# One decoder step on one core: the order of loads and combinations in the output projection, the order of the memory attention's matmuls, two splits through PSUM, and POOL's sums in halves

## The chip, the core and the metric

The kernel runs on one core of a Trainium2 chip. A core has a matmul engine (TensorE, here PE, whose weight loads are listed as PEld), a vector engine (VectorE, DVE), an activation engine (ScalarE, ACT), a general engine (GpSimd, POOL) and a queue engine that mostly issues transfers (SyncE, SP). Each works through its own list of instructions in order, and waits on semaphores for the others. SBUF is the on-chip memory, PSUM the smaller one into which PE accumulates. The metric is the device time of one execution in microseconds (us), lower is better.

## What is computed

One inference step of a decoder layer, for a prompt of 512 tokens and 8 sample sequences of 4 tokens (544 columns in all, handled as two halves of 272):

```python
def decoder_layer(x, s0, k_buf, v_buf, mem_k, mem_v, lb, ...):
    y, s_new, k_new, v_new = token_mixer(rmsnorm(x, norm_mix_w), s0, k_buf, v_buf, ...)
    x = x + y                                   # ends with concat([a_out, b_out]) @ w_out
    x = x + memory_attend(rmsnorm(x, norm_xattn_w), mem_k, mem_v, w_mq, w_mo)
    x = x + swiglu(rmsnorm(x, norm_ffn_w), w_gate, w_up, w_down)
```

The token mixer projects x, runs a gated recurrence with 8 heads (HGRN) and sliding-window attention side by side, and projects both together with w_out (2048 x 2048). The memory attention has 4 heads of 128 over 256 memory rows for the prompt and over caches for the samples, and a projection w_mo from 512 to 2048. The feed-forward part has 5632 hidden units. All is in float32.

## The kernel before

**Products.** A float32 product is made as three products of rounded operands: each operand is split into a high part (a cast on ScalarE) and a low part (the rest, a subtraction on VectorE), and PE does high x high, high x low and low x high. The large projections are in addition done with seven block products in place of eight: `B11, B21, T2, T1, T3, B22, T4` of `QO`, whose weight operands are blocks A11, A21, A12, A22 of the weight matrix and their combinations S1, S2, S3 and A12 less S2, and whose data operands are blocks of the columns and combinations of them.

**Stages.** Input projection with the HGRN heads in between (`hgrn_head`, which puts other work between its own steps with `draw(n)`: n matmuls of whatever stands in the list `line`), then the output projection, the memory attention, its projection w_mo (called mo), gate and up, down, final norm. Each of these lays its operands down while the stage before still runs.

**Output projection** (`out_unit`). A unit is one quarter of the output columns (o4) of one half of the inner dimension: rows1 with o4 = 0, 2, 3, 1, then rows2 with 2, 3, 0, 1. It loads its four blocks through `load` (512 KB each, SP's queue, tiles `oraw`), makes S1, S2, S3 on POOL with `comb` (tiles `ocomb`), and then, product by product, splits the weights (`ohi` and `oh2` on ScalarE, `olo` on VectorE), lets PE do 24 matmuls, and adds the result into x. Blocks come from pool `wr` with 4 buffers, but A22, once the second half is under way, from pool `wx` with 2. While the unit o4 = 1 of rows1 runs, its hook `rows2_parts` builds the data operands of rows2: `Rows` makes a combination into `ot1` and one into `mix0` on POOL (L634, L635), `part` splits each operand (`split`, L606 on ScalarE and L607 on VectorE) and makes two more combinations (L645, L647). In the units of rows2 the hook `beside` prepares operands of the memory attention. The order of each engine's list comes from a scheduler, out of the program's order and the waits that it expects, not from the order of the code alone.

**Memory attention.** Query projections `mq` for four heads and two halves stand in `line`; the scores of each follow after `draw` calls. The first units of mo stand in `line` too, so that they can run between the last heads. `add_mo(i, half)` is one unit of mo: 24 matmuls over three part products (`at`) and four heads (k), then the addition into x (DVE, L1556), the square (`sqt`) and its sum, on POOL for the first half (`SS`, L1562) and on VectorE for the second (`SW`).

**Operands of gate and up** (`ffn_parts`). After the units of mo that finish two rows of x, the data operands are made: `B11` and `B21` with their high part on ScalarE (`ffn_w`) and their low part on VectorE (L1583), further ones f and t (L1535, L1589) on VectorE and POOL. `norm_rows` makes the norms' factors in two halves, each with `rsqrt`, which loads ScalarE's table set first.

Of the kernel before, what the change touches and what calls it, by code (L numbers as in the profile page):

```python
# [10 lines left out]
F32 = mybir.dt.float32  # L11
# [8 lines left out]
P = 128  # L20
# [24 lines left out]
def hybrid_step(ctx: ExitStack, tc: tile.TileContext, a):  # L45
# [863 lines left out]
    def hgrn_head(h):  # L909
# [7 lines left out]
        qp = hg.tile([P, TT], F32, tag="qp", name="qp")  # L917
        nc.gpsimd.tensor_tensor(qp, q, f, ALU.mult)
        step()
        draw(8)  # L920


        A = hg.tile([P, NB, P], F32, tag="A", name="A")
# [160 lines left out]
    def out_unit(rows, o4, old, hook=None):  # L1084

        n0 = o4 * 4 * P

        def load(f, c, last=False):
            p, n = (wx[0], 2) if rows2_on and last else (wr, 4)
            t = p.tile([P, WCH * P], F32, tag="raw", name="oraw", bufs=n)  # L1090
            t = t.rearrange("p (k c) -> p k c", k=DN)
            c0 = n0 + c * 2 * P
            dma(t, w_out[f * P : (f + DN) * P, c0 : c0 + 2 * P].rearrange("(k p) c -> p k c", p=P))
            return t

        def comb(x, y, op):
            t = wst.tile([P, WCH * P], F32, tag="raw", name="ocomb", bufs=3)
            t = t.rearrange("p (k c) -> p k c", k=DN)
            nc.gpsimd.tensor_tensor(t, x, y, op)
            return t  # L1100

        f0 = rows.g * 4
        A11, A21, A12, A22 = load(f0, 0), load(f0, 1), load(f0 + DN, 0), load(f0 + DN, 1, True)

        def run():
            S1 = comb(A21, A22, ALU.add)
            S2 = comb(S1, A11, SPLIT)
            S3 = comb(A21, A11, SPLIT)
            accs = [acc_tile("o_ps") for _ in range(2)]
            if next(units_made) % 2:  # L1110
                accs.reverse()
            o, x = (
                {
                    q: y[:, 2 * i : 2 * i + 2, t]
                    for q, (i, t) in dict(c11=(0, T0), c12=(0, T1), c21=(1, T0), c22=(1, T1)).items()
                }
                for y in (old, X[o4])
            )
            for i, (q, src, bank, first, dst, fresh) in enumerate((
                ("B11", A11, 0, True, "c11", True), ("B21", A12, 1, True, "c11", False),  # L1120
                ("T2", S2, 0, False, "c12", True), ("T1", S1, 1, True, "c22", True),
                ("T3", S3, 0, False, "c22", False), ("B22", None, 1, False, "c12", False),
                ("T4", A22, 0, False, "c21", True),
            )):
                rows.part(i)
                if src is None:
                    src = comb(A12, S2, SPLIT)
                hi = wst.tile([P, WCH * P], F32R, tag="hi", name="ohi")
                lo = wst.tile([P, WCH * P], F32R, tag="lo", name="olo")
                hi, lo = (t.rearrange("p (k c) -> p k c", k=DN) for t in (hi, lo))  # L1130
                if heads_done:
                    for j in range(2):
                        js = slice(2 * j, 2 * j + 2)
                        h2 = ps_to[0].tile([P, 2, 2 * P], F32R, tag="to"[j], name="oh2")
                        if j == 0:
                            nc.scalar.copy(hi, src)
                        nc.scalar.copy(h2, src[:, js])
                        nc.vector.tensor_tensor(lo[:, js], src[:, js], h2.bitcast(F32), SPLIT)  # L1138
                else:
                    split(hi, lo, src)  # L1140
                rows.part(i + 1)
                if hook:
                    hook(i)
                xh, xl = rows.ops[q]
                acc = accs[bank]
                for wt, xt_, at in ((hi, xh, 0), (hi, xl, 1), (lo, xh, 2)):
                    for p in range(2):
                        s = slice(p * P, (p + 1) * P)
                        for k in range(DN):
                            nc.tensor.matmul(  # L1150
                                acc[:, p, :HT], wt[:, k, s], xt_[:, k],
                                start=first and k + at == 0, stop=k == DN - 1 and at == 2,
                                skip_group_check=True,
                            )
                            if at != 1 or k % 2:
                                yield
                add(x[dst], (o if fresh else x)[dst], acc[:, :, :HT])

        return run()
# [67 lines left out]
    def norm_rows(out, sums, tag="t"):  # L1227

        for (b, e), s in zip(HALF, sums):
            pt = ps("nr_ps", tag)[:, : TT // 2]  # L1230
            n = s.shape[1]
            for u in range(n):
                nc.tensor.matmul(pt, ones, s[:, u], start=u == 0, stop=u == n - 1)
            v = small.tile([P, TT], F32, tag="nv", name="nv", bufs=1)[:, : TT // 2]
            nc.vector.tensor_scalar(v, pt, 1.0 / D, EPS, ALU.mult, ALU.add)
            t = small.tile([P, TT], F32, tag="sqt", name="nt", bufs=2)[:, : TT // 2]
            rsqrt(out[:, b:e], v, t)

    rows2 = []

# [263 lines left out]
    for n, u in enumerate(units):  # L1504
        need(("mq", *u))
        if n:
            x_turn(*units[n - 1])
            draw(4)
        else:
            draw(36)  # L1510
        x_scores(*u)
        draw(14)
        if n:
            x_values(*units[n - 1])
        for _ in range(6 if n >= MH - 1 else 0):
            x_more(1)
            draw(5)
# [21 lines left out]
    def add_mo(i, half, done=None):  # L1539


        def run():
            if i not in mo_w:
                mo_w[i] = [next(wparts) for _ in range(MH)]
            acc = acc_tile("mo_ps")
            for at in range(3):
                for k, hi, lo in mo_w[i]:
                    wt, xt_ = (hi, hi, lo)[at], ox[half][k][at % 2]
                    for u in range(2):
                        nc.tensor.matmul(  # L1550
                            acc[:, u, :HT], wt[:, u * P : (u + 1) * P], xt_,
                            start=k + at == 0, stop=k == MH - 1 and at == 2,
                        )
                        yield
            x = X[i // 2][:, 2 * i % 4 : 2 * i % 4 + 2, (T0, T1)[half]]
            nc.vector.tensor_tensor(x, x, acc[:, :, :HT], ALU.add)  # L1556
            if i == 0:
                nc.scalar.activation(S3[half], x, AF.Square)
            else:
                t = post.tile([P, 2, HT], F32, tag="sqt", name="sqt", bufs=2)  # L1560
                nc.scalar.activation(t, x, AF.Square)
                (nc.vector if half else nc.gpsimd).tensor_add(S3[half], S3[half], t)  # L1562
            if done:
                done(i)

# [9 lines left out]
    def ffn_parts(i):  # L1575
# [3 lines left out]
        for u, q in enumerate(("B11", "B21")):  # L1579
            o = 2 * i + u  # L1580
            hi, lo = (t[:, i] for t in fops[q])
            ffn_w(hi, o, T0)
            nc.vector.scalar_tensor_tensor(  # L1583
                lo, xt(o)[:, T0], vcol("ffn", o), hi.bitcast(F32), ALU.mult, SPLIT
            )
        t1 = ap.tile([P, HT], F32, tag="t1", name="t1", bufs=2)
        t2 = ap.tile([P, HT], F32, tag="t2", name="t2")
# [545 lines left out]
```

## Time and profile before

| | |
|---|---|
| median of 3 runs | 2591.98 us (2590.53 to 2594.45) |
| the profiled execution | 2587.27 us, span 2585.5 us, mean granted clock 0.993 |
| PE busy | 2511.4 us, 97 % of the span |
| VectorE, ScalarE, POOL busy | 66 %, 60 %, 43 % |
| output projection | about 780 to 974 us of the span |
| memory attention and mo | about 974 to 1136 us |

The span runs from the first to the last instruction. All times of rows below are in us from its start, within this one execution. A number in square brackets at the end of a row is the time for which the engine had been idle, with what ended the wait.

### The profile page before, as it was taken

What the parts mean: (1) busy time and instruction counts of PE and PEld (TensorE: products, weight loads), DVE (VectorE), ACT (ScalarE), POOL (GpSimd) and SP (SyncE); (2) the same over time, 40 slices, a digit from 0 to 9 for tenths busy, and PEclk for the clock granted to TensorE, in tenths of its full rate; (3) what the DMA queues carried; (4) which work ended last, traced back from release to release, by engine and by line L of the source; (5) the groups of instructions that cost most, each with busy time, mean ns of one, the idle gap of its engine ahead of it and who ended that gap; (6) DMA issues with size and microseconds to landing.
All of it is one profiled execution on the core that took longest, in us unless ns stands there. A gap on an engine that the chain in (4) does not pass through costs nothing.

```text
span 2585.5 us, 48037 instructions
## 1 busy us (share of the span) xinstructions
PE 2511.4 (97%) x19679; PEld 2443.3 (95%) x19679; DVE 1708.9 (66%) x2560; ACT 1557.7 (60%) x2181; POOL 1104.3 (43%) x643
## 2 busy tenths in 40 slices
PE   8999999999999999989999999999999999999997
PEld 7999999998998998779999999999999999999987
DVE  5555655565559796497666666666666676777887
ACT  5343223333327685467677777777776778767767
POOL 4101122122125631165555555555555566665752
PEclk9999999999999999999999999999999999999999
DMA  7222323554524226523333333333333453333325
GB/s 240 83 68 82 91 83 92 152 149 143 182 66 135 91 73 186 187 93 107 116 107 117 114 123 113 122 115 113 116 107 116 142 211 133 101 131 133 116 70 164
DMA packets 287164, 315.44 MB, mean 122 GB/s; under 512 B 9508, under 2 KB 239220, under 8 KB 284097
## 3 DMA queue, kind: packets, MB, share of 16 engines
q1 hardware_dynamic: 273024, 264.80, 32.2%
q0 software_dynamic: 13920, 47.58, 5.6%
q8 instruction: 155, 2.54, 0.4%
q14 instruction: 65, 0.52, 0.1%
HBM read 278.28 MB, written 33.64 MB: 121 GB/s over the span
## 4 chain that ended last, share of the span: by engine, by line
PE 54%; DVE 6%; ACT 3%; issue 2%; DMA 2%; POOL 1%; ACTq 0%; DVEq 0%; POOLq 0%; SPq 0%
PE s_ps L1703 48%; PE o_ps L1150 3%; PE d_ps L1987 1%; PE mq_ps L1445 1%; DVE slo L1647 1%; DMA wraw<-in_w_down_dram 1%; DVE wlo L132 1%; ACT shi L1645 0%; ACT h L1646 0%; DVE x L1887 0%; DMA xkv<-in_cache_mem_v_dram 0%; POOL scomb L1665 0%; DVE olo L1138 0%; DMA wraw<-in_w_mq_dram 0%; PE xk_ps L1363 0%
## 5 line engine op out<-in xcount | busy, mean ns | idle before, releaser
L1647 DVE TENSOR_TENSOR slo<-scomb,h 128x1024 fp32r<-128x1024 f32 x256 | 312.5, 1221 | 243.2 <-ACT h L1646 232.8
L1645 ACT CAST shi<-scomb 128x1024 fp32r<-128x1024 f32 x256 | 269.2, 1052 | 190.8 <-PE s_ps L1703 168.9
L131 ACT CAST whi<-wraw 128x1024 fp32r<-128x1024 f32 (+1 forms) x204 | 169.4, 845 | 342.0 <-PE in_ps L345 278.4
L1665 POOL TENSOR_TENSOR scomb<-sraw 128x1024 f32<-128x1024 f32 (+1 forms) x134 | 319.4, 2386 | 7.5 <-DVE slo L1647 2.5
L1665 POOL TENSOR_TENSOR scomb<-sraw,scomb 128x1024 f32<-128x1024 f32 (+1 forms) x67 | 166.5, 2486 | 327.9 <-DVE slo L1647 319.3
L1645 ACT CAST shi<-sraw 128x1024 fp32r<-128x1024 f32 x192 | 201.6, 1050 | 160.9 <-issue 99.5
L345 PE MATMUL in_ps<-xh,whi 128*128 128x272 f32 x1280 | 276.6, 297 | 0.8 <-ACT whi L131 0.8
L345 PE MATMUL in_ps<-xl,whi 128*128 128x272 f32 x1280 | 274.2, 295 | 0.0
L345 PE MATMUL in_ps<-xh,wlo 128*128 128x272 f32 x1280 | 272.1, 294 | 0.9 <-DVE wlo L132 0.8
L132 DVE TENSOR_TENSOR wlo<-wraw,whi 128x1024 fp32r<-128x1024 f32 (+1 forms) x204 | 208.0, 1033 | 96.6 <-ACT whi L131 92.1
L1646 ACT CAST h<-scomb 128x1024 fp32r<-128x1024 f32 x256 | 258.6, 1010 | 3.1 <-DVE slo L1647 3.0
L1647 DVE TENSOR_TENSOR slo<-sraw,h 128x1024 fp32r<-128x1024 f32 x192 | 233.8, 1218 | 28.0 <-ACT h L1646 23.2
L345 PEld LDWEIGHTS in_ps<-xh,whi 128*128 128x128 f32 x1280 | 201.8, 189 | 6.6 <-issue 4.3
L345 PEld LDWEIGHTS in_ps<-xh,wlo 128*128 128x128 f32 x1280 | 201.9, 189 | 6.4 <-issue 4.4
L345 PEld LDWEIGHTS in_ps<-xl,whi 128*128 128x128 f32 x1280 | 202.0, 189 | 5.1 <-issue 4.4
L1646 ACT CAST h<-sraw 128x1024 fp32r<-128x1024 f32 x192 | 194.1, 1011 | 17.8 <-DVE slo L1647 17.6
L1703 PE MATMUL s_ps<-T,shi 128*128 128x272 f32 x1408 | 191.9, 288 | 0.9 <-DVE T L607 0.5
L1703 PEld LDWEIGHTS s_ps<-T,shi 128*128 128x128 f32 x1408 | 182.8, 188 | 1.5 <-ACT T L606 0.8
L611 DVE TENSOR_TENSOR gu<-gu,s_ps 128x272 f32<-128x272 f32 x264 | 111.3, 435 | 109.4 <-PE s_ps L1703 106.8
L1703 PE MATMUL s_ps<-dT,shi 128*128 128x272 f32 x1280 | 173.8, 288 | 2.7 <-ACT h L1646 1.4
L1703 PEld LDWEIGHTS s_ps<-dT,shi 128*128 128x128 f32 x1280 | 165.1, 188 | 3.6 <-ACT h L1646 1.6
L1665 POOL TENSOR_TENSOR scomb<-scomb,sraw 128x1024 f32<-128x1024 f32 (+1 forms) x67 | 160.4, 2395 | 4.2
(523 smaller groups left out, 5723.6 us busy)
## 6 DMA issues: line engine op xcount, KB each, us to landing
sraw<-in_w_gate_dram SPq DMA_DIRECT2D x44, 1024.0 KB, 5.1
sraw<-in_w_up_dram SPq DMA_DIRECT2D x44, 1024.0 KB, 5.1
wraw<-in_w_in_dram SPq DMA_DIRECT2D x84, 512.0 KB, 4.0
sraw<-in_w_down_dram SPq DMA_DIRECT2D x40, 1024.0 KB, 5.2
oraw<-in_w_out_dram SPq DMA_DIRECT2D x32, 512.0 KB, 3.9
h_d<-gu POOLq DMA_DIRECT2D x22, 544.0 KB, 4.6
wraw<-in_w_mk_dram SPq DMA_DIRECT2D x16, 512.0 KB, 3.7
wraw<-in_w_mv_dram SPq DMA_DIRECT2D x16, 512.0 KB, 3.9
```

Source lines behind the costliest of these rows:

```text
L131: nc.scalar.copy(hi[:, s], raw[:, s])
L132: nc.vector.tensor_tensor(lo[:, s], raw[:, s], hi[:, s].bitcast(F32), SPLIT)
L345: nc.tensor.matmul(acc[:, i, : e - b], wt, xt[:, b:e], start=j + at == 0, stop=j == KD - 1 and at == 2,)
L611: nc.vector.tensor_tensor(out, x, y, ALU.add)
L1150: nc.tensor.matmul(acc[:, p, :HT], wt[:, k, s], xt_[:, k], start=first and k + at == 0, stop=k == DN - 1 and at == 2, skip_group_check=True,)
L1445: nc.tensor.matmul(acc, wt, xt_, start=j + at == 0, stop=j == KD - 1 and at == 2)
L1645: first = nc.scalar.copy(hi, src)
L1646: nc.scalar.copy(h2, src)
L1647: return first, nc.vector.tensor_tensor(lo, src, h2.bitcast(F32), SPLIT)
L1665: ins = nc.gpsimd.tensor_tensor(t[:, p], x[:, p], y[:, p], op)
L1703: nc.tensor.matmul(accs[p], wt[:, k, s], xt_[:, k], start=k + at == 0, stop=k == n - 1 and at == 2,)
L1987: nc.tensor.matmul(acc[:, 0, : e0 - b0], (hi, hi, lo)[at], hp[k][at % 2][:, b0:e0], start=k + at == 0, stop=k == nf - 1 and at == 2,)
```

## The change

Seven places are changed.

- HGRN heads 0 and 7 draw 16 matmuls in place of 8 at one of their steps.
- In units of the output projection with a hook, A22 is loaded third and from pool `wr`, A12 fourth. Units without one keep their order.
- The instructions that a hook makes on POOL are put behind the instruction that makes S3 (`tc.issue_after(summed.ins)` ties those of the same engine alone).
- The second half of each norm in `norm_rows` no longer loads the table set.
- The memory attention draws 47 matmuls in place of 36 ahead of the first scores.
- The first two units of mo order their 24 matmuls by head, and by part product within a head.
- `ffn_parts` writes the high parts of B11 and B21 a second time, into PSUM, and the splits on VectorE read them there; POOL's sums of squares are made in two halves of 272 columns.

```diff
-        draw(8)
+        draw(8 if 0 < h < H - 1 else 16)
...
-            nc.gpsimd.tensor_tensor(t, x, y, op)
-            return t
+            return t, nc.gpsimd.tensor_tensor(t, x, y, op)
...
-        A11, A21, A12, A22 = load(f0, 0), load(f0, 1), load(f0 + DN, 0), load(f0 + DN, 1, True)
+        A11, A21 = load(f0, 0), load(f0, 1)
+        if hook:
+            A22 = load(f0 + DN, 1)
+            A12 = load(f0 + DN, 0)
+        else:
+            A12, A22 = load(f0 + DN, 0), load(f0 + DN, 1, True)
...
-            S1 = comb(A21, A22, ALU.add)
-            S2 = comb(S1, A11, SPLIT)
-            S3 = comb(A21, A11, SPLIT)
+            S1, _ = comb(A21, A22, ALU.add)
+            S2, _ = comb(S1, A11, SPLIT)
+            S3, summed = comb(A21, A11, SPLIT)
...
-                    hook(i)
+                    with tc.issue_after(summed.ins):
+                        hook(i)
...
-            rsqrt(out[:, b:e], v, t)
+            rsqrt(out[:, b:e], v, t, preload=b == 0)
...
-            draw(36)
+            draw(47)
...
-            for at in range(3):
-                for k, hi, lo in mo_w[i]:
-                    wt, xt_ = (hi, hi, lo)[at], ox[half][k][at % 2]
-                    for u in range(2):
...
+            order = [(at, part) for at in range(3) for part in mo_w[i]]
+            if done is None and i < 2:
+                order.sort(key=lambda o: o[1][0])
+            for n, (at, (k, hi, lo)) in enumerate(order):
...
-                (nc.vector if half else nc.gpsimd).tensor_add(S3[half], S3[half], t)
+                if half:
+                    nc.vector.tensor_add(S3[half], S3[half], t)
+                else:
+                    for u in range(2):
+                        nc.gpsimd.tensor_add(S3[half][:, u], S3[half][:, u], t[:, u])
...
+            h2 = ps_to[0].tile([P, 512], F32R, tag="to"[u], name="b2")[:, :HT]
+            ffn_w(h2, o, T0)
             ffn_w(hi, o, T0)
             nc.vector.scalar_tensor_tensor(
-                lo, xt(o)[:, T0], vcol("ffn", o), hi.bitcast(F32), ALU.mult, SPLIT
+                lo, xt(o)[:, T0], vcol("ffn", o), h2.bitcast(F32), ALU.mult, SPLIT
             )
```

**Where instructions stand.** POOL in the output projection, before the change: 8850 to 8856 are the blocks of the unit o4 = 3 of rows1, 9108 to 9114 those of o4 = 1, and A22 of the latter is 9114.

```order
L634 TENSOR_TENSOR ot1_9167<-mix0_406 128x1088
L635 TENSOR_TENSOR mix0_406<-mix0_406,mix1_407 128x4x272
L645 TENSOR_TENSOR mix0_406<-mix0_406 128x4x272
L1099 TENSOR_TENSOR ocomb_8858<-oraw_8852,oraw_8856 128x1024
L1099 TENSOR_TENSOR ocomb_8860<-ocomb_8858,oraw_8850 128x1024
L1099 TENSOR_TENSOR ocomb_8862<-oraw_8852,oraw_8850 128x1024
L1099 TENSOR_TENSOR ocomb_9036<-oraw_8854,ocomb_8860 128x1024
L1099 TENSOR_TENSOR ocomb_9116<-oraw_9110,oraw_9114 128x1024
L1099 TENSOR_TENSOR ocomb_9118<-ocomb_9116,oraw_9108 128x1024
L1099 TENSOR_TENSOR ocomb_9120<-oraw_9110,oraw_9108 128x1024
L647 TENSOR_TENSOR mix1_407<-mix1_407,mix0_406 128x4x272
```

POOL at the same place with the change.

```order
L1099 TENSOR_TENSOR ocomb_8858<-oraw_8852,oraw_8856 128x1024
L1099 TENSOR_TENSOR ocomb_8860<-ocomb_8858,oraw_8850 128x1024
L1099 TENSOR_TENSOR ocomb_8862<-oraw_8852,oraw_8850 128x1024
L1099 TENSOR_TENSOR ocomb_9036<-oraw_8854,ocomb_8860 128x1024
L1099 TENSOR_TENSOR ocomb_9116<-oraw_9110,oraw_9112 128x1024
L1099 TENSOR_TENSOR ocomb_9118<-ocomb_9116,oraw_9108 128x1024
L1099 TENSOR_TENSOR ocomb_9120<-oraw_9110,oraw_9108 128x1024
L634 TENSOR_TENSOR ot1_9167<-mix0_406 128x1088
L635 TENSOR_TENSOR mix0_406<-mix0_406,mix1_407 128x4x272
L645 TENSOR_TENSOR mix0_406<-mix0_406 128x4x272
L647 TENSOR_TENSOR mix1_407<-mix1_407,mix0_406 128x4x272
```

The three operations of the hook moved from the front of the unit o4 = 3 to behind S3 (ocomb_9120) of the unit o4 = 1, whose S1 (ocomb_9116) now reads oraw_9112; the load of oraw_9112 waits for ocomb_9036, the last reader of the tile that had the buffer.

ScalarE around the cast oT3_9508, before the change: the casts of 8854 are those of B21 in the unit o4 = 3.

```order
L1136 CAST ohi_8900<-oraw_8854 128x1024
L1137 CAST oh2_8902<-oraw_8854 128x512
L1137 CAST oh2_8906<-oraw_8854 128x512
L606 CAST oT3_9508<-mix0_406 128x1088
L1136 CAST ohi_8934<-ocomb_8860 128x1024
```

ScalarE around the same cast with the change: the casts of 9108 are those of B11 in the unit o4 = 1, the casts of 9114 those of B21.

```order
L1141 CAST oh2_9126<-oraw_9108 128x512
L1140 CAST ohi_9124<-oraw_9108 128x1024
L1141 CAST oh2_9130<-oraw_9108 128x512
L606 CAST oT3_9508<-mix0_406 128x1088
L1141 CAST oh2_9160<-oraw_9114 128x512
L1140 CAST ohi_9158<-oraw_9114 128x1024
L1141 CAST oh2_9164<-oraw_9114 128x512
```

The cast, which reads what L635 writes, moved by one unit, from between B21 and T2 of the unit o4 = 3 to between B11 and B21 of the unit o4 = 1.

PE where mo starts beside the last head of the memory attention, with the change: 11615 and 11642 are the first two units of mo, oxh00 to oxh20 and oxl00 to oxl20 the operands of the first three heads, xt and xo steps of the last head.

```order
L1557 MATMUL mo_ps_11642<-oxl10_10516,whi_11611 128x272 x2
L1557 MATMUL mo_ps_11642<-oxh10_10515,wlo_11612 128x272 x2
L1557 MATMUL mo_ps_11642<-oxh20_10517,whi_11611 128x272
L1481 MATMUL xt_ps_11591<-ident_78,p_11524 128x128 x4
L1557 MATMUL mo_ps_11642<-oxh20_10517,whi_11611 128x272
L1557 MATMUL mo_ps_11642<-oxl20_10518,whi_11611 128x272 x2
L1557 MATMUL mo_ps_11642<-oxh20_10517,wlo_11612 128x272 x2
L1492 MATMUL xo_ps_11598<-pT_11596,vm__10511 128x256 x2
L1557 MATMUL mo_ps_11615<-oxh30_10519,whi_11605 128x272 x2
```

Before, only the products high x high of the first three heads, 12 matmuls, stand ahead of the last head's oxh30; now all three part products do, 36 matmuls.

## Rows read from the trace of the kernel before

**Rows 1.** The page, its first part: busy time, share of the span, instructions.
```profile
PE 2511.4 (97%) x19679; PEld 2443.3 (95%) x19679; DVE 1708.9 (66%) x2560; ACT 1557.7 (60%) x2181; POOL 1104.3 (43%) x643
```

**Rows 2.** Waits of PE: us in total, times, longest us.
```profile
PE mo_ps L1550 <- DVE x L1556: 7.8, 5, 2.8
```

**Rows 3.** Windows: length, busy us (instructions) by engine, granted clock, DMA share, GB/s.
```profile
840.00:860.00 20.00, 16.30 (x118) 16.09 (x117) 10.78 (x17) 11.14 (x16) 16.08 (x8) 0.91 0.26 84
```

**Rows 4.** Timeline of PE in the out projection: start, us, instruction, idle before.
```profile
847.98 2.75 PE L1150 MATMUL o_ps<-oT,ohi 128*128 128x272 f32 x16 [3.69 <-ACT ohi L1136]
...
852.34 2.44 PE L1150 MATMUL o_ps<-oT,ohi 128*128 128x272 f32 x16
...
864.69 2.18 PE L1150 MATMUL o_ps<-oB,ohi 128*128 128x272 f32 x16
...
867.71 2.18 PE L1150 MATMUL o_ps<-oB,ohi 128*128 128x272 f32 x16
```

**Rows 5.** Timeline of POOL, the same stretch.
```profile
832.27 2.55 POOL L634 TENSOR_TENSOR ot<-mix 128x1088 f32<-128x1088 f32 x1
834.90 3.47 POOL L635 TENSOR_TENSOR mix<-mix,mix 128x1088 f32<-128x1088 f32 x1
838.45 2.58 POOL L645 TENSOR_TENSOR mix<-mix 128x1088 f32<-128x1088 f32 x1
841.96 2.47 POOL L1099 TENSOR_TENSOR ocomb<-oraw 128x1024 f32<-128x1024 f32 x1 [0.94 <-DMA oraw<-in_w_out_dram]
...
851.91 2.40 POOL L1099 TENSOR_TENSOR ocomb<-oraw,ocomb 128x1024 f32<-128x1024 f32 x1 [2.74 <-issue]
```

**Rows 6.** Timeline of DVE, the same stretch.
```profile
833.41 2.57 DVE L607 TENSOR_TENSOR oB<-mix,oB 128x1088 fp32r<-128x1088 f32 x1
...
840.88 1.29 DVE L607 TENSOR_TENSOR oT<-mix,oT 128x1088 fp32r<-128x1088 f32 x1 [0.27 <-ACT oT L606]
842.10 0.71 DVE L611 TENSOR_TENSOR x<-x,o_ps 128x544 f32<-128x544 f32 x1
```

**Rows 7.** Transfers between 854.2 and 858.2: KB each, us from issue to landing.
```profile
oraw<-in_w_out_dram SPq DMA_DIRECT2D x1, 512.0 KB, 3.5
```

**Rows 8.** Timeline of ACT, the same stretch.
```profile
839.75 1.10 ACT L606 CAST oT<-mix 128x1088 fp32r<-128x1088 f32 x1
...
863.94 1.05 ACT L1136 CAST ohi<-oraw 128x1024 fp32r<-128x1024 f32 x1
```

**Rows 9.** Timeline of POOL, third unit of the second half.
```profile
917.43 2.76 POOL L1099 TENSOR_TENSOR ocomb<-oraw,ocomb 128x1024 f32<-128x1024 f32 x1 [11.49 <-issue]
```

**Rows 10.** Timeline of PE, third unit of the second half.
```profile
933.65 2.16 PE L1150 MATMUL o_ps<-oB,ohi 128*128 128x272 f32 x16
```

**Rows 11.** Timeline of DVE in the last HGRN head.
```profile
778.76 3.45 DVE L607 TENSOR_TENSOR oT<-mix,oT 128x1088 fp32r<-128x1088 f32 x1
```

**Rows 12.** Timeline of PE at the start of the memory attention.
```profile
991.09 1.10 PE L1465 MATMUL xs_ps<-kmT,qx 128*128 128x256 f32 x4 [2.33 <-issue]
```

**Rows 13.** Timeline of PE in the mo projection.
```profile
1071.68 1.09 PE L1476 MATMUL xt_ps<-ident,p 128*128 128x128 f32 x4 [1.92 <-DVE oxl L1339]
...
1114.35 1.26 PE L1550 MATMUL mo_ps<-oxh,whi 128*128 128x272 f32 x8 [2.85 <-DVE x L1556]
```

**Rows 14.** Groups of DVE from 1097 to 1141: count, busy us, mean ns.
```profile
L1583 DVE SCALAR_TENSOR_TENSOR B11l<-x,vec,B11h 128x272 fp32r<-128x272 f32 x6 | 7.3, 1221 | 0.1
...
L1583 DVE SCALAR_TENSOR_TENSOR B21l<-x,vec,B21h 128x272 fp32r<-128x272 f32 x5 | 5.1, 1022 | 0.0
```

**Rows 15.** Timeline of DVE in the mo projection.
```profile
1110.59 2.73 DVE L1535 SCALAR_TENSOR_TENSOR f<-x,vec,t 128x272 f32<-128x272 f32 x1
...
1126.56 0.49 DVE L1583 SCALAR_TENSOR_TENSOR B11l<-x,vec,B11h 128x272 fp32r<-128x272 f32 x1
```

**Rows 16.** Timeline of POOL in the mo projection.
```profile
1110.04 2.98 POOL L1808 TENSOR_TENSOR f<-f,f 128x1088 f32<-128x1088 f32 x1
```

**Rows 17.** Timeline of ACT in the gate stage.
```profile
1174.44 1.28 ACT L77 ACT_TABLE_LOAD   x1
```

More of the change, by code (lines that the diff above doesn't have):

```diff
@@ L1126, in run @@
                 if src is None:
-                    src = comb(A12, S2, SPLIT)
+                    src, _ = comb(A12, S2, SPLIT)
                 hi = wst.tile([P, WCH * P], F32R, tag="hi", name="ohi")
@@ L1545, in run @@
             acc = acc_tile("mo_ps")
-            for at in range(3):
-                for k, hi, lo in mo_w[i]:
-                    wt, xt_ = (hi, hi, lo)[at], ox[half][k][at % 2]
-                    for u in range(2):
[L1550 to L1554, printed above, removed]
+            order = [(at, part) for at in range(3) for part in mo_w[i]]
+            if done is None and i < 2:
+                order.sort(key=lambda o: o[1][0])
+            for n, (at, (k, hi, lo)) in enumerate(order):
+                wt, xt_ = (hi, hi, lo)[at], ox[half][k][at % 2]
+                for u in range(2):
+                    nc.tensor.matmul(
+                        acc[:, u, :HT], wt[:, u * P : (u + 1) * P], xt_,
+                        start=n == 0, stop=n == len(order) - 1,
+                    )
+                    yield
             x = X[i // 2][:, 2 * i % 4 : 2 * i % 4 + 2, (T0, T1)[half]]
@@ L1561, in run @@
                 nc.scalar.activation(t, x, AF.Square)
-                (nc.vector if half else nc.gpsimd).tensor_add(S3[half], S3[half], t)
+                if half:
+                    nc.vector.tensor_add(S3[half], S3[half], t)
+                else:
+                    for u in range(2):
+                        nc.gpsimd.tensor_add(S3[half][:, u], S3[half][:, u], t[:, u])
             if done:
```

## The prediction

> **What bounds the kernel now.** The page comes first: PE is busy for 97 % of the span [rows 1], so work on the other engines costs time only where PE stands still for it, and a change of order can gain no more than PE's gaps around it. The list of PE's waits says which stage holds them: the largest entry is the mo projection, where products wait five times, 7.8 us in all, for VectorE's addition into x [rows 2]. The table of windows then shows that a gap can cost twice: around 850 us the granted clock is 0.91 of full speed [rows 3]. The timeline of PE there shows how: behind a gap of 3.69 us the next product of 24 matmuls takes from 847.98 to 852.34, 4.36 us, where one later takes from 864.69 to 867.71, 3.02 us [rows 4]. So 1.3 us are lost behind the gap, at the lower of the clock's two levels, 1.2 in place of 2.4 GHz, for part of them.
>
> **Out projection, before the hook's unit.** The 3.69 us end with ScalarE's casts of S2, so with POOL: in front of S1 it does the three operations of L634, L635 and L645, then waits 0.94 us for A22 [rows 5]. The change takes the three away from this place. What is left is A22's load; its issue stands behind the split oB, which VectorE does in 2.57 us beside POOL, while a split of the same shape takes 1.29 alone [rows 6]. So the load comes some 1.3 us sooner, and so does the product: **-1.3** (bounds -0.5, if the load is slow for other reasons, and -2.5, with the load of 9114 gone from the queue ahead as well). Left over is a gap of some 2.4 us.
>
> **Out projection, the hook's unit (o4=1 of rows1).** Two edits meet here. A22 (oraw_9112) now lives in the buffer that the last combination of the unit before (ocomb_9036) reads, and the three moved operations stand behind S3, which stands behind S1, which needs A22. In the times of before: that combination ends at 851.91 + 2.40 = 854.3 [rows 5]; a load landed 3.5 us after its issue there [rows 7], so A22 at 857.8. S1, S2 and S3 at 2.4 each: 865.0. L634 2.55: 867.6. L635, at the 2.6 of its neighbours rather than its own 3.47: 870.2. ScalarE's order has the cast oT3_9508, which reads L635's result, ahead of the casts for B21, and so it stands still until then: 1.10 for that cast, half of 1.05 for the first half cast (an estimate), 1.05 for B21's hi [rows 8], which gives 872.9 where B21's product began at 867.71 [rows 4]: 5.2 late. VectorE adds to it: its half of the split oT3 meets POOL's L645 (870.2 to 872.8), takes 1.29 after that, and the addition that frees B21's PSUM bank (0.71 [rows 6]) is queued behind it: 874.8. I take **+7.1**, the later of the two, with 5.2 as the lower bound and 8.5 as the upper (POOL's and VectorE's operations blocking each other once more, as L635's 3.47 against 2.6 shows).
>
> Behind that wait A12's load (9114) is hidden. In two later units, the third and fourth of rows2, nothing hides it: A12 takes a buffer that the unit's own S3 frees, and A22 one that the last combination of the unit before frees. Third unit: that combination ends at 917.43 + 2.76 = 920.2 [rows 9]; load 3.5, S1 to S3 7.2: 930.9; A12's load 3.5: 934.4; half cast and hi 1.6: 936.0, and B21's product began at 933.65 [rows 10]: 2.4 late. With POOL at 2.76 for each, 3.4. I take 2.9 for each of the two units: **+5.8** (4.8 to 6.8). Each of the three new gaps is as long as those after which matmuls ran slowly, or longer, at 1.3 us each: **+4.0** (0 to 4.5).
>
> **HGRN heads.** Twice as many matmuls of other work are put early into heads 0 and 7. That moves steps of head 7: on VectorE the splits oT2 and oT1 now stand ahead of the updates of S for which PE waits. Before, such a split took 3.45 us beside POOL [rows 11]. One of them would be caught by the six matmuls between: **+2** (from -1, if the extra matmuls fill waits in head 0, to +4).
>
> **Memory attention and the start of mo.** PE ran out of matmuls 2.33 us ahead of the first scores [rows 12]; 11 more, at 3.02/24 = 0.126 us each, are 1.4 us: **-1.0** (0 to -1.4). With the first two units ordered by head, 36 matmuls in place of 12 need only the first three heads. That is 24 × 0.126 = 3.0 us of work beside the gap of 1.92 us ahead of the last head's transposes [rows 13] and the three short ones after it: **-2.5** (0 to -4.5, the second with the slow matmuls there gone).
>
> **mo projection.** B11l and B21l took 1221 and 1022 ns in the mean [rows 14] and 0.49 us where POOL stood [rows 15]: 6 × 0.73 + 5 × 0.53 = 7.0 us of waiting. POOL is what they wait for; beside it an addition with one operand in PSUM takes its usual 0.71 [rows 5, 6], and the change gives both splits such an operand. But the largest gap, 2.85 us at 1114.35 [rows 13], ends behind f, which took 2.73 beside POOL's 2.98 [rows 15, 16], has both operands in SBUF and stays as it is. So I take **-3** (0, if all of the waiting moves on to f, t and SW, to -8). The Trainium skill's page "SBUF — State Buffer", section "Who interferes with whom", says that VectorE with two SBUF inputs and GpSimd share a port pair as an exclusive lock, while one SBUF input leaves it free; the rows agree. By that rule all of the 7.0 goes, and the sum would be 4.0 lower. The four copies for h2 and POOL's sums in halves lie on engines with idle time here; the first h2 copy of the gate stage now shares its PSUM bank with the last of these, **+1** (0 to 3.5).
>
> **Second norm.** One table load less on ScalarE, 1.28 us [rows 17], in a stretch where PE waits for what comes behind it: **-1.3** (0 to -3).
>
> **Sum.** -1.3 + 7.1 + 5.8 + 4.0 + 2 - 1.0 - 2.5 - 3 + 1 - 1.3 = +10.8. The profiled execution took 2587.27 us, so 2598.1; the median of the three runs shown is 2591.98, 4.7 higher, so **2602.8**. A measurement of this kernel can tell about 0.2 % (5.2 us) from no change.
>
> **The rivals.** *The out projection hides the new waits* (ends on the other side). If the loads and combinations come so much earlier that the three gaps shrink to less than 1 us in all, 7.1 + 5.8 + 4.0 fall away: -6.1, 2585.9, faster. For it: the one wait for a load that POOL shows around this place is 0.94 us [rows 5]. Against it: from ocomb_9036's start to B21's operand I count 872.9 - 851.9 = 21.0 us, and PE has 867.7 - 851.9 = 15.8 us of products; both start at the same event, so coming earlier helps nothing. It decides from a chain under 17 us. 0.10. *The mo projection gets all of it back*: all of the 7.0, and with VectorE that much ahead the whole 7.8 of its waits, -7.8 in place of -3, and the start of mo -4.5 in place of -2.5: +4.0, 2596.0, within 0.2 %. For it: VectorE is one queue, so what B11l saves reaches f. Against it: f's own wait. 0.14. *More is lost*: the waits of the mo projection only move on (0 in place of -3), head 7 costs 4, and the gate's start 3.5: +18.3, 2610.3. For it: VectorE had next to no idle time before these splits [rows 14]. 0.14. The forecast itself, 2597 to 2608, has 0.62.
>
> **How the numbers follow.** Slower by over 0.2 % means above 2597.2: 0.62 less a little at its lower end, and the third rival, 0.74. Faster (below 2586.8): the first rival and a little of the second, 0.11. Within: 0.15. The range reaches from 2591, which leaves out the first rival and some of the second, to 2613, which takes in the third. The forecast's own range is 2597 to 2608.
>
> **What would show it.** Right: on POOL L634, L635 and L645 in a row behind three combinations in the fourth unit, on ScalarE a wait of some 5 us ahead of oT3's cast, a PE gap of about 7 us ahead of a B product, and two of about 3 us in the third and fourth units of rows2, each with slow matmuls behind it; in the mo projection B11l and B21l at about 0.5 us, and f and SW no shorter. Wrong: PE gaps in the out projection under 1 us, or a mo projection without gaps.

## The result

The changed kernel takes 2610.47 us in the median of four runs (2608.17 to 2615.19), the kernel before 2591.26 in as many (2586.95 to 2594.45). The ratio is 1.0078, with a 95 % interval from 1.0057 to 1.0098: 0.8 % slower, 19.2 us between the medians. The forecast was slower, 2603 with a range from 2591 to 2613. The two profiled executions lie near opposite ends of their runs (2587.27 of before, 2615.19 of after, span 2613.4), so their spans differ by more than the medians do; gaps are compared below, not spans.

### The profile after

The first part of the page (as [rows 1]). PE does as many matmuls as before, in more time.

```profile
PE 2522.1 (97%) x19679; PEld 2455.1 (94%) x19679; DVE 1697.8 (65%) x2560; ACT 1561.6 (60%) x2195; POOL 1100.9 (42%) x650
```

PE's waits (as [rows 2]): us in total, times, longest.

```profile
PE o_ps L1155 <- DVE x L611: 11.4, 4, 8.7
PE o_ps L1155 <- ACT ohi L1140: 8.8, 4, 2.5
PE s_ps L1716 <- ACT shi L1658: 5.7, 4, 4.1
PE mo_ps L1557 <- DVE x L1563: 5.7, 3, 3.3
```

The output projection now heads the list. PE's timeline there (as [rows 4, 10]): start, us, instruction, idle before.

```profile
854.41 2.29 PE L1155 MATMUL o_ps<-oT,ohi 128*128 128x272 f32 x16 [1.77 <-ACT ohi L1140]
...
881.55 3.67 PE L1155 MATMUL o_ps<-oB,ohi 128*128 128x272 f32 x16 [8.75 <-DVE x L611]
...
951.89 3.13 PE L1155 MATMUL o_ps<-oB,ohi 128*128 128x272 f32 x16 [2.48 <-ACT ohi L1140]
...
978.56 2.28 PE L1155 MATMUL o_ps<-oB,ohi 128*128 128x272 f32 x16 [2.51 <-ACT ohi L1140]
```

The gap of 3.69 us has become 1.77. Ahead of B21 of the unit o4 = 1 of rows1 there is one of 8.75 us, and the 24 matmuls behind it take from 881.55 to 886.05, 4.50 us in place of 3.0. In the third and fourth units of rows2 B21 waits 2.48 and 2.51 us; behind the first of these the product takes 4.64 (951.89 to 956.53), behind the second 3.12 (978.56 to 981.68). The windows of these three products (as [rows 3], the granted clock is the third number from the end) show the clock's lower level for part of the first two, and the full 2.4 GHz throughout the third:

```profile
881.55:886.05 4.50, 4.50 (x24) 4.50 (x25) 3.86 (x6) 4.02 (x6) 0.00 (x0) 0.65 0.00 0
951.89:956.53 4.64, 4.64 (x24) 4.64 (x25) 4.17 (x7) 4.64 (x8) 0.00 (x0) 0.63 0.09 30
978.56:981.68 3.12, 3.12 (x24) 3.12 (x25) 2.65 (x5) 3.12 (x6) 0.00 (x0) 1.00 0.00 0
```

POOL, ScalarE and VectorE ahead of the long gap (as [rows 5 to 8]):

```profile
858.58 2.42 POOL L1099 TENSOR_TENSOR ocomb<-oraw,ocomb 128x1024 f32<-128x1024 f32 x1 [2.96 <-issue]
864.82 2.40 POOL L1099 TENSOR_TENSOR ocomb<-oraw 128x1024 f32<-128x1024 f32 x1 [3.82 <-DMA oraw<-in_w_out_dram]
...
874.58 2.48 POOL L635 TENSOR_TENSOR mix<-mix,mix 128x1088 f32<-128x1088 f32 x1
877.13 2.49 POOL L645 TENSOR_TENSOR mix<-mix 128x1088 f32<-128x1088 f32 x1
```

```profile
877.08 1.10 ACT L606 CAST oT<-mix 128x1088 fp32r<-128x1088 f32 x1 [9.70 <-POOL mix L635]
```

```profile
878.21 2.55 DVE L607 TENSOR_TENSOR oT<-mix,oT 128x1088 fp32r<-128x1088 f32 x1 [9.50 <-ACT oT L606]
880.69 0.71 DVE L611 TENSOR_TENSOR x<-x,o_ps 128x544 f32<-128x544 f32 x1
```

The reader sees the chain of the prediction, link by link: the last combination of the unit before ends at 861.0, S1 starts when the load has landed (3.82 us of idle time), S2, S3 and the two operations of `Rows` follow without a break until 877.06, ScalarE has stood still for 9.70 us and casts oT3, VectorE's split of it takes 2.55 beside L645, and the addition behind that ends the gap at 881.4. From the start of that combination to PE's start it is 881.55 - 858.58 = 23.0 us; the forecast was 874.8 - 851.9 = 22.9.

The groups of VectorE in the mo projection (as [rows 14, 15]): count, busy us, mean ns, idle before.

```profile
L1540 DVE SCALAR_TENSOR_TENSOR f<-x,vec,t 128x272 f32<-128x272 f32 x5 | 6.4, 1270 | 2.8 <-POOL t L1602 2.8
...
L1596 DVE SCALAR_TENSOR_TENSOR B11l<-x,vec,b 128x272 fp32r<-128x272 f32 x6 | 2.9, 491 | 0.7 <-ACT b L1537 0.7
```

B11l is at 0.49 us in the mean, and so is B21l; f, with both operands in SBUF, is at 1.27 (1.14 in the stretch of [rows 14]). Ahead of f VectorE now stands idle for 2.8 us until POOL's t is there, where before it did for 0.3: part of the time saved on the splits goes into this wait. PE's other gaps (as [rows 12, 13]):

```profile
785.85 0.80 PE L1035 MATMUL ho_ps<-qp,S 128*128 128x128 f32 x2 [3.34 <-DVE S L1021]
...
1016.91 1.14 PE L1470 MATMUL xs_ps<-kmT,qx 128*128 128x256 f32 x4 [4.13 <-issue]
...
1111.45 1.26 PE L1557 MATMUL mo_ps<-oxh,whi 128*128 128x272 f32 x8 [1.84 <-ACT whi L131]
...
1180.55 0.77 PE L1716 MATMUL s_ps<-B,shi 128*128 128x272 f32 x4 [4.08 <-ACT shi L1658]
```

Those of 3.34 (for S in the last head), 1.84 (for the weights of the third unit of mo) and 4.08 us (in the gate stage) were not there before; the one of 1.92 us beside the last head of the memory attention [rows 13] is gone.

### The profile page after: what moved, and what is told of

The parts are those of the page before. It is cut to its first block, busy times and chain, and to the rows that moved or that the text cites. A ratio compares the mean times of both kernels' runs of the same rounds, so it can differ in the third digit from the quotient of the medians.

```text
span 2613.4 us, 48045 instructions
## 1 busy us (share of the span) xinstructions
PE 2522.1 (97%) x19679; PEld 2455.1 (94%) x19679; DVE 1697.8 (65%) x2560; ACT 1561.6 (60%) x2195; POOL 1100.9 (42%) x650
## 4 chain that ended last, share of the span: by engine, by line
PE 54%; DVE 5%; issue 3%; POOL 2%; ACT 2%; DMA 1%; ACTq 0%; POOLq 0%; DVEq 0%
PE s_ps L1716 48%; PE mq_ps L1450 2%; PE d_ps L2000 1%; POOL ocomb L1099 1%; PE o_ps L1155 1%; DVE slo L1660 1%; DMA oraw<-in_w_out_dram 1%; POOL scomb L1678 1%; DVE olo L1142 0%; DMA wraw<-in_w_down_dram 0%; ACT shi L1658 0%; ACT h L1659 0%; DMA xkv<-in_cache_mem_v_dram 0%; DVE x L1900 0%; DVE wlo L132 0%
```

## The experiments

Twelve kernels: the kernel before with parts of the change, or the changed kernel with parts of it taken back, each timed beside the kernel before. Microseconds of difference are between the two medians. The ratio is worked out from all runs and can differ from the quotient of the medians by some 0.05 % (1.3 us).

### Output projection alone

```diff
 kernel before
+        if hook:
+            A22 = load(f0 + DN, 1)
+            A12 = load(f0 + DN, 0)
...
+                    with tc.issue_after(summed.ins):
+                        hook(i)
```

> The kernel before with the two edits of the output projection alone (A22 third and from wr in units with a hook; the hook's POOL operations behind S3). Theory, that these two carry the loss: a PE gap of 8 to 9 us ahead of B21 of the unit o4 = 1, two of about 2.5 us in the third and fourth units of rows2, one of about 2 us where before had 3.69; 13 to 19 us slower than before. Rival, that the loss comes as much from the early draws in the heads, the memory attention and the gate's start: at most 9 us slower.

Measured: 2609.94 us against 2592.05, 17.9 slower, ratio 1.0070 (1.0057 to 1.0083).

```profile
847.28 3.35 PE L1155 MATMUL o_ps<-oT,ohi 128*128 128x272 f32 x16 [3.00 <-ACT ohi L1140]
...
874.14 3.97 PE L1155 MATMUL o_ps<-oB,ohi 128*128 128x272 f32 x16 [7.05 <-DVE x L611]
...
944.98 2.28 PE L1155 MATMUL o_ps<-oB,ohi 128*128 128x272 f32 x16 [3.06 <-ACT ohi L1140]
...
956.81 3.53 PE L1155 MATMUL o_ps<-oT,ohi 128*128 128x272 f32 x16 [2.55 <-DVE x L611]
...
971.57 2.28 PE L1155 MATMUL o_ps<-oB,ohi 128*128 128x272 f32 x16 [0.99 <-ACT ohi L1140]
```

The long gap is 7.05 us here; ahead of B21 in rows2 they are 3.06 and 0.99, and there is one of 2.55 ahead of a T product, where VectorE's addition into x comes late; before had 0.71 in that place. Behind 3.06 us of standing still 24 matmuls run at the usual rate here, behind 2.55 they don't. The expectation had the long gap at 8 to 9 us, which it is not without the rest of the change. Two edits in one function carry nearly the whole loss.

### The order of loads alone, and the tie behind S3 alone

The first and the second half of the diff above.

> The kernel before with the order of loads alone (A22 third and from wr). Theory: the hook's POOL operations are early, so nothing waits for them; the two gaps of about 2.5 us in rows2 are there, each with up to 1.3 us of slow matmuls behind it, and the gap of 3.69 us ahead of the T2 product of o4 = 3 stays within 0.7: 4 to 9 us slower. Rival, that the late A22 stalls the unit o4 = 1 by itself: a gap of over 4 us there and over 9 us in all.

> The kernel before with the tie behind S3 alone. Theory: A22 is early, so S3 ends some 3.5 us sooner than with both edits, but the scheduler puts the cast of oT3 one product earlier, ahead of B11's hi; the chain from the last combination (2.4 + 7.2 + 5.0 + 1.1 + 1.0) is 16.7 us, PE has four products or 12.1 us: a gap of 4 to 6 us ahead of B11 of o4 = 1, none in rows2, 2 us less where before had 3.69; 2 to 6 us slower. Rival, that the tie does what frees POOL and costs nothing: no gap over 1.5 us in the unit, and 1 to 3 us faster.

Measured: the loads alone 2604.84 us, 12.8 slower (1.0052, 1.0039 to 1.0064); the tie alone 2598.48, 6.4 slower (1.0025, 1.0012 to 1.0039). Together 19.2, where both in one kernel cost 17.9: the two losses add up, within their intervals.

```profile
874.42 2.28 PE L1155 MATMUL o_ps<-oB,ohi 128*128 128x272 f32 x16 [2.94 <-ACT ohi L1141]
...
889.64 3.67 PE L1155 MATMUL o_ps<-oB,ohi 128*128 128x272 f32 x16 [2.38 <-DVE x L611]
...
958.00 3.74 PE L1155 MATMUL o_ps<-oT,ohi 128*128 128x272 f32 x16 [2.50 <-DVE x L611]
```

```profile
848.59 4.00 PE L1150 MATMUL o_ps<-oT,ohi 128*128 128x272 f32 x16 [3.64 <-ACT ohi L1135]
...
869.99 3.39 PE L1150 MATMUL o_ps<-oB,ohi 128*128 128x272 f32 x16 [3.85 <-ACT ohi L1135]
```

```profile
867.89 1.10 ACT L606 CAST oT<-mix 128x1088 fp32r<-128x1088 f32 x1 [5.77 <-POOL mix L635]
```

With the loads alone, A12's wait shows in a third place, 2.94 us in the unit o4 = 1 of rows1 (874.42), which in the changed kernel hides under the long gap, and two additions into x come late (889.64, 958.00). The kernel before has both of these gaps too, shorter:

```profile
881.48 2.25 PE L1150 MATMUL o_ps<-oB,ohi 128*128 128x272 f32 x16 [1.53 <-DVE x L611]
...
943.52 2.25 PE L1150 MATMUL o_ps<-oT,ohi 128*128 128x272 f32 x16 [0.71 <-DVE x L611]
```

So neither theory had its size right: no gap of over 4 us in that unit, yet 12.8 us in all. With the tie alone ScalarE waits 5.77 us for L635 and PE 3.85, one product earlier, as expected, and more is lost than the gap: the 24 matmuls behind it take from 869.99 to 874.62, 1.6 us more than at the usual rate. In front of that, at 848.59, nothing was gained: 3.64 us, though the hook's operations were out of POOL's way.

### The buffer of A22

```diff
 loads alone
-            A22 = load(f0 + DN, 1)
+            A22 = load(f0 + DN, 1, True)
```

> The kernel before with A22 created third and A12 fourth in units with a hook, but A22 from pool wx as before. Theory, that the buffer in wr is the whole cost of the new order of loads: the loads wait for nothing late, no gap over 2 us in the second half of the output projection but those of before, within 2 us of before. Rival, that the place of the loads in SP's queue costs: 5 us or more slower.

Measured: 2591.21 us against 2592.37, ratio 0.9998 (0.9987 to 1.0009): no change. The order of the tiles is that of the kernel with the loads alone, the buffer that of before. The buffer is the whole of the 12.8 us, as far as the interval (3.4 us faster to 2.3 slower) can tell: in it A22 waits for no reader of the unit before. SP issues it at 834.4 here and at 831.8 in the kernel before, in the changed kernel at 861.0.

### The changed kernel without both edits of the output projection

> The changed kernel with both edits of the output projection undone. Theory: none of the gaps of 8.75, 2.48 and 2.51 us; what is left is the wait for S in the last head (3.3 us), 1.8 us more ahead of the first scores, 6 us less from the start of mo to the gate, 4 us more at the gate's start: 0 to 6 us slower than before. Rival: 9 or more slower.

Measured: 2596.00 us against 2592.05, ratio 1.0018 (1.0009 to 1.0027): 4.0 slower. The rest of the change loses by itself as well. The gap ahead of T2 of the unit o4 = 3 is 5.21 us here: POOL does L634, L635 and L645 in front of S1, until 849.98. In the changed kernel, which differs in the two edits alone, POOL has nothing in front of S1, which waits for its load until 848.4, and the gap is 1.77. The parts of the rest one by one:

### Early draws, in two heads and in one

```diff
-        draw(8)
+        draw(8 if 0 < h < H - 1 else 16)      # first kernel
+        draw(8 if h else 16)                   # second kernel
```

> The kernel before with the early draws of heads 0 and 7 alone. Theory: in the last head the wait for S (3.2 us) and one more for kp (1.7 us) appear, as in the two kernels that have this edit so far: 3 to 6 us slower. Rival, that those waits only take the place of others in the head and in the out projection behind it: within 2 us of before.

> The kernel before with 16 early matmuls in head 0 alone. Theory, that the loss of the draws comes from head 7, where VectorE's splits for the output projection stand ahead of S: no wait for S, within 1.5 us of before. Rival: head 0 has a share of 2 us or more in the loss of 3.8.

Measured: both heads 2596.07 us against 2592.29, 3.8 slower (1.0018, 1.0009 to 1.0027); head 0 alone 2590.62 against 2592.37 (0.9997, 0.9986 to 1.0007), no change. PE and VectorE in the last head of the first kernel:

```profile
784.40 0.49 PE L1035 MATMUL ho_ps<-qp,S 128*128 128x128 f32 x2 [3.10 <-DVE S L1021]
...
824.26 0.77 PE L1150 MATMUL o_ps<-oT,ohi 128*128 128x272 f32 x4 [2.05 <-ACT ohi L1136]
...
856.55 3.62 PE L1150 MATMUL o_ps<-oT,ohi 128*128 128x272 f32 x15 [5.21 <-ACT ohi L1136]
```

```profile
779.22 4.80 DVE L607 TENSOR_TENSOR oT<-mix,oT 128x1088 fp32r<-128x1088 f32 x1 [0.23 <-ACT oT L606]
784.05 0.29 DVE L1021 COPY S<-hk_ps 128x128 f32<-128x128 f32 x1
```

The split oT stands ahead of S and takes 4.80 us; PE waits 3.10 for S. Two waits for ScalarE follow in the output projection, 2.05 and 5.21 us, the latter where before had 3.69 [rows 4]. The loss is head 7's, by difference: no run has the draws in head 7 alone.

### Draws ahead of the first scores, and the table load

> The kernel before with 47 matmuls ahead of the first scores and without the second table load of each norm. Theory: what comes before the scores is the chain of the second norm, so the 11 matmuls end sooner or later beside the same gap of 2.3 to 2.5 us, and the load lay beside other work: 1.5 us faster to 1.5 us slower. Rival, as forecast: 2.3 us faster, the gap down to 1.0 to 1.4 us.

Measured: 2592.03 us against 2592.29, ratio 1.0000 (0.9991 to 1.0009): no change. The gap ahead of the scores is 2.41 us. For the draws, a count of the matmuls of mq ahead of the first scores shows why, before (first line) and here (second line):

```profile
973.50:991.00 17.50, 13.86 (x96) 13.02 (x96) 0.47 (x2) 1.00 0.87 272
```

```profile
973.50:991.00 17.50, 13.86 (x96) 13.02 (x96) 0.44 (x2) 1.00 0.86 268
```

There are 96 in both (and in the changed kernel). The 11 more stand behind the first scores: the second ones start at 994.43, where before it was 992.95. So the edit puts no matmul ahead of the gap, and what 11 more there would do is not tested. What ends the gap can be read from ScalarE and VectorE:

```profile
986.91 1.05 ACT L131 CAST whi<-wraw 128x1024 fp32r<-128x1024 f32 x1 [2.17 <-DMA wraw<-in_w_mq_dram]
```

```profile
990.56 0.82 DVE L1453 TENSOR_TENSOR qx<-mq_ps,R 128x288 f32<-128x288 f32 x2
```

The scores (991.11) read qx, and VectorE makes qx with the norm's factor R, whose second half stands on ScalarE (987.86) behind a cast that waits 2.17 us for a weight's transfer. Before, that cast starts at 986.89, with the table load (984.82 to 986.10) and a wait of 0.78 us in front of it: the load had lain in the wait. In the kernel with head 0's draws alone, which has neither edit, that cast waits 2.77 us for the transfer and the gap is 4.32, so the 4.13 us of the changed kernel need no cause in the change. The transfer took 8.7 us from issue to landing before, 10.7 in the kernel with head 0's draws and 10.5 in the changed one; why it was slower in those executions stays open.

### The first two units of mo by head

```diff
+            if done is None and i < 2:
+                order.sort(key=lambda o: o[1][0])
```

> The kernel before with the first two units of mo ordered by head, and nothing else. Theory: the gaps of 1.92, 0.73 and 0.46 us beside the last head are filled, and the matmuls there run faster; none comes in their place: 2 to 5 us faster. Rival: the weights of the third unit come late, a gap of about 1.8 us for ScalarE's cast as in the changed kernel: within 1.5 us of before.

Measured: 2586.12 us against 2592.29, 6.2 faster (4.9 by the ratio), ratio 0.9981 (0.9972 to 0.9990). Its median is the lowest of all. PE in a window around the last head, before (first line) and here (second line):

```profile
1060.00:1080.00 20.00, 15.75 (x142) 11.77 (x141) 5.65 (x15) 4.53 (x13) 2.19 (x3) 0.83 0.61 203
```

```profile
1060.00:1080.00 20.00, 18.20 (x194) 14.29 (x187) 6.40 (x17) 4.88 (x14) 4.46 (x6) 1.00 0.63 207
```

PE is busy for 18.20 of these 20 us in place of 15.75, at a full granted clock in place of 0.83. Of the gaps of 1.92, 0.73 and 0.46 us beside the last head, only that of 0.46 ahead of oxh is left.

### The splits through PSUM and POOL's halves

```diff
 kernel before
...
+            h2 = ps_to[0].tile([P, 512], F32R, tag="to"[u], name="b2")[:, :HT]
+            ffn_w(h2, o, T0)
...
+                lo, xt(o)[:, T0], vcol("ffn", o), h2.bitcast(F32), ALU.mult, SPLIT
```

> The kernel before with the two splits through PSUM and POOL's sums in halves alone. Theory: B11l and B21l at about 0.5 us, the waits for x in mo down from 8 to 5 or 6 us, and a gap of about 4 us in the gate stage that before did not have, behind a combination on POOL that waits for VectorE: 0 to 3 us slower. Rival, that the mo projection gets all of its waits back and the gate's start costs nothing: 5 to 8 us faster.

Measured: 2594.51 us against 2592.29, 2.2 slower (3.4 by the ratio), ratio 1.0013 (1.0004 to 1.0022).

```profile
PE mo_ps L1550 <- DVE x L1556: 5.2, 2, 3.1
```

```profile
1157.56 0.80 PE L1709 MATMUL s_ps<-B,shi 128*128 128x272 f32 x4 [4.09 <-ACT shi L1651]
```

```profile
1140.39 1.22 DVE L1653 TENSOR_TENSOR slo<-sraw,h 128x1024 fp32r<-128x1024 f32 x1 [0.28 <-ACT h L1652]
```

```profile
1151.85 4.58 POOL L1671 TENSOR_TENSOR scomb<-sraw,scomb 128x512 f32<-128x512 f32 x2 [9.35 <-DVE slo L1653]
```

The copy h on ScalarE that the first split of gate's weights reads, in the kernel before:

```profile
1081.69 1.00 ACT L1646 CAST h<-sraw 128x1024 fp32r<-128x1024 f32 x1
```

Waits for x in mo fall from 7.8 us [rows 2] to 5.2, in two gaps in place of five, and those two, 3.08 and 2.11, stay near the lengths of before's (2.85 and 2.48). The gap of 4.09 us is in the gate stage: the first copy h shares its PSUM bank with the b2 tiles. Before, it ran at 1081.69, long ahead; now it runs at 1139.36, and the split, which before started at 1132.48, at 1140.39, the splits behind that one are late in turn, and POOL's first long combination, which has waited 9.35 us for them, ends late and with it ScalarE's shi.

### The splits for six of eight pairs, and the rest with them

```diff
 first two units of mo by head
+            if i < KH - 2:
+                h2 = ps_to[0].tile([P, 512], F32R, tag="to"[u], name="b2")[:, :HT]
+                ffn_w(h2, o, T0)
+            else:
+                h2 = hi
```

> The kernel before with the first two units of mo ordered by head, and the splits through PSUM for the first six of eight pairs of rows only. Theory, that the late first copy h2 of the gate stage, behind the last b2 in the same PSUM banks, makes the gap of 4.1 us: that gap is gone, mo waits less for x than in the kernel with the order alone, 6 to 10 us faster than before. Rival, that the splits through PSUM gain nothing even so: not faster than the order alone (5 us faster than before), or the third unit's weights late by 1.8 us.

> The same with all else of the change that cost nothing by itself: POOL's halves, 47 matmuls ahead of the first scores, no second table load, 16 early matmuls in head 0. Theory: these add nothing that a measurement can tell, within 2 us of the kernel without them. Rival: POOL's halves or the draws cost 2 us or more.

Measured: 2589.24 us against 2592.37, ratio 0.9987 (0.9974 to 0.9999), and 2588.01, ratio 0.9986 (0.9975 to 0.9998). So 3 to 4 us faster than before, and not faster than the order alone: the rival, though the intervals of the three kernels overlap.

```profile
1087.83 1.91 PE L1552 MATMUL mo_ps<-oxh,whi 128*128 128x272 f32 x8 [1.84 <-ACT whi L131]
...
1146.69 1.27 PE L1710 MATMUL s_ps<-T2h,shi 128*128 128x272 f32 x8 [1.61 <-ACT gu L1731]
...
1156.37 0.52 PE L1710 MATMUL s_ps<-B,shi 128*128 128x272 f32 x2 [1.52 <-ACT shi L1652]
```

```profile
1086.73 1.04 ACT L131 CAST whi<-wraw 128x1024 fp32r<-128x1024 f32 x1
...
1125.26 1.01 ACT L1653 CAST h<-sraw 128x1024 fp32r<-128x1024 f32 x1
```

The first copy h is early again, at 1125.26, and the gap of 4.09 us is down to 1.52, so that half of the theory holds: what made h late was the last b2 tiles. But a gap of 1.61 us has come up 10 us ahead of it (1146.69), which before doesn't have and the kernel with all the splits through PSUM has at 0.2 us, so the two still make 3.1 us. And together with the order by head the copies make ScalarE late with the third unit's weights: the cast whi runs at 1086.73, behind four copies of 0.47 us, PE waits 1.84 us and its next eight matmuls take until 1089.53, 1.70 in place of 1.0. Neither the order alone nor the splits alone has this wait; the changed kernel has it, at 1111.45. The last kernel shows that the draws, the table load and POOL's halves add nothing that can be told.

## Why the prediction was right

The direction and the main cause were right: the output projection alone loses 17.9 of the 19.2 us. The size was too low: 2610.5 lies in the range, but above the forecast's own 2597 to 2608, and the sum was +10.8. The number of the rival *More is lost* (2610.3) is all but met, which is partly luck: head 7 and the gate's start lost what it says, but the waits of the mo projection did fall, from 7.8 us to 5.7, and the start of mo gained more than the 2.5 us that this rival leaves it. Of the terms, these are what the runs make of them:

- *Out projection, before the hook's unit* (-1.3): nothing for the tie alone, which leaves 3.64 us of the 3.69, and 0.7 for both edits (3.00). The step that failed is that the split oB would end 1.3 us sooner without POOL beside it. In the kernel with the tie alone it does run in 1.29 us, but starts at 834.98, where before had 833.41; the load is issued no sooner, at 837.5 against 837.2. In the changed kernel the term was too small: there the draws make POOL's three operations the longer wait, and taking them away brings the gap from 5.21 to 1.77 us.

```profile
834.98 1.29 DVE L607 TENSOR_TENSOR oB<-mix,oB 128x1088 fp32r<-128x1088 f32 x1
```

- *The hook's unit* (+7.1, 5.2 to 8.5): 7.05 us with the output projection alone, 8.75 in the changed kernel, just above the bound. The mechanism is shown by three kernels: the tie alone gives 3.85 us one product earlier, the loads alone 2.94 for A12 in its place, and A22 in its old buffer nothing.
- *A12 in two later units* (+5.8): 2.48 and 2.51 us in the changed kernel, 3.06 and 0.99 with the output projection alone, where an addition into x is late by 2.55 as well. Not foreseen: later additions into x, 2.38 and 2.50 us with the loads alone where before had 1.53 and 0.71. In the changed kernel they are 1.35 and 1.03, hardly more than before. Why VectorE is late with them wasn't tried.
- *Slow matmuls* (+4.0): 1.5 us behind the first of the three new gaps, 1.6 behind the second, 0.1 behind the third: 3.2. How much is lost behind a gap is also a matter of the execution. In the kernel with A22 in its old buffer, PE has the same matmuls and a gap of 3.71 us in the place of before's 3.69, and the 24 matmuls behind it take 5.61 us (850.58 to 856.19) in place of 4.36.
- In sum the output projection was forecast at +15.6 and measured at +17.9 alone. That these are so near is partly luck: the gain of 1.3 was hardly there, and the later additions had no term.
- *HGRN heads* (+2): +3.8, all of it head 7 by difference. The wait for S was named; the cost behind it, 5.21 us where before had 3.69, was not.
- *Memory attention* (-1.0) and *second norm* (-1.3): 0 together, by the kernel with both. The step that failed for the first is that 11 more matmuls would stand ahead of the first scores: the 96 there are the same with 36 and with 47, and the others stand behind. I had also read PE's gap, which says "issue", as a lack of matmuls; the chain that ends last there is a weight's transfer, ScalarE's cast behind it, and the norm behind that. For the second, that PE waits in the gate stage for what stands behind the load: without it the two gaps there are 1.88 and 1.40 us, where they were 1.95 and 1.46. On the table load the Trainium skill's page "ScalarE: Activation LUTs", section "What ACT_TABLE_LOAD costs", gives 1283 ns and 1380 more for a drain. The load's 1.28 us [rows 17] agree; a drain does not show, since the next instruction starts 1.30 us after the load did; and taking one away gave nothing that can be told here, no more than 0.1 us of either gap.
- *Start of mo* (-2.5, to -4.5): -6.2 alone (-4.9 by the ratio, interval from -2.6 to -7.3, 0.10 % to 0.28 %). The bound with the slow matmuls gone was nearer than the number taken. In the changed kernel part of it goes back, 1.84 us for the third unit's weights.
- *mo projection* and *the gate's start* (-3 and +1): +2.2 together. The 2.6 us of waits for x that were gained agree with -3; the gate's start costs 4.1 us of gap, above its bound of 3.5. So the rule that one operand in PSUM doesn't contend with POOL held in all 16 splits of the changed kernel: 0.48 to 0.50 us, where the means were 1.22 and 1.02, though 13 of them run beside an operation of POOL. (The 0.49 us of [rows 15] is no case of POOL standing still: its t runs beside that split for the last 0.26 us.) The rival that all of the waiting comes back fell: two long waits stay, ahead of which f, with two operands in SBUF, still takes 1.27 us in the mean. The step that failed is that the four copies for h2 cost nothing because their engine has idle time: together with the order by head they made ScalarE late with the third unit's weights, 1.84 us.

The parts timed alone, 17.9 + 3.8 - 0.3 - 6.2 + 2.2, make 17.4 us; the whole change measures 19.2. By the ratios it is 21.3 and 20.2. Without the output projection the parts make -0.5, or 3.2 by the ratios, where the kernel with all of them measured 4.0, or 4.7. These differences are within the intervals. They hide two interactions that the traces show, of opposite sign: order with splits (1.84 us more) and early draws with the output projection's edits (a gap of 1.77 us in place of 5.21).

## What to carry to other kernels

Ahead of an edit that moves a load, ask which buffer it takes and who reads that buffer last: a load that was ahead by a whole unit became one link of a chain of 23 us against 16 us of PE's work, and the same order with the old buffer cost nothing. An operation that is tied behind another to get it out of the way needs the same question for everything queued behind its results, here a cast in ScalarE's queue that stood in front of the next product's operand. And a gap counts more than its length where matmuls run slowly behind it, so filling two short gaps, as the order by head did, can bring more than the gaps say.

## What was not expected of the hardware

Matmuls behind a gap were slow in some places and not in others, in one execution: 4.50 us for 24 behind 8.75 us of standing still, 4.64 behind 2.48, but 3.12 behind 2.51. The granted clock goes with it: 0.65, 0.63 and 1.00.

The length of the gap alone doesn't decide: with the output projection alone there is a full clock behind 3.06 us, and 0.59 behind 2.55 (956.81 to 961.00). What told the last two of the changed kernel apart is not shown by these runs.
